# Two-matmul attention scores, recurrence states on 128 rows, a conv norm without its wide reciprocal, and weight low parts made by ScalarE and an accumulating DMA

## The chip, the cores and the metric

The kernel runs on one core of one Trainium2 chip. Its time is the device time of one execution in microseconds (us). Three runs of the kernel before gave 1368.75, 1370.97 and 1372.02 us, a median of 1370.97. The profile shows one further execution, of 1370.76 us, whose span on the engines is 1369.0 us.

## The reference, cut to what matters

Two layers work on a residual stream of 512 tokens by 1024 channels, all in float32. Each layer norms the stream (RMSNorm, modulated by a conditioning vector), projects it to 28 column tiles of 128, runs three token mixers on those tiles, projects the mixers' outputs back, and then runs a gated MLP with a depthwise convolution of width 3.

```python
for l in range(DEPTH):                      # 2 layers
    mod = cond @ w_ada[l] + b_ada[l]        # six shifts, scales and gates
    h = _rmsnorm(x, norm1_w[l]) * (1.0 + sc1) + sh1
    x = x + g1 * _token_mixers(h, ...)      # conv | attention | HGRN2, then w_out
    h = _rmsnorm(x, norm2_w[l]) * (1.0 + sc2) + sh2
    x = x + g2 * _conv_ffn(h, w_up[l], conv_f_w[l], w_down[l])
return _rmsnorm(x, final_norm_w)

# in _token_mixers
a = _depthwise_conv(a_val * sigmoid(a_gate), conv_w, conv_b)      # 256 channels, width 31
a = silu(_layernorm(a, ln_w, ln_b))
att: 6 heads of 64; scores q.k / 8 minus a slope times distance, three dilated windows
rec: 6 heads of 64, both directions; state = decay * state + k^T v, chunk after chunk
return concatenate([a, att, rec]) @ w_out
```

## The kernel before

**Precision.** TensorE's fast type (`float32r`) keeps fewer bits than float32, so every weight and every activation of the large products is split into a high part `hi` (the value rounded to that type) and a low part `lo` (value minus `hi`). A product is then three matmuls, hi·hi, hi·lo and lo·hi, into one PSUM tile (`block`). Weights come from HBM in chunks of 128 rows by up to 1024 columns. `loader` brings them into raw buffers (`wr`, three of them), and `splitter` makes `hi` by a copy on ScalarE or VectorE, whichever the planner thinks sooner done, and `lo` by a subtraction on VectorE. A chunk is split when it lies at most three chunks ahead of the one in use (five for the wide ones).

**Stages.** Each layer has: `first_group`, in which the first column tiles (six) are accumulated at the same time, row block by row block, as the normed activations `h[k]` appear; then one tile after the other (`tile_gemm`, 24 matmuls of 512 columns for 8 row blocks). In the mixers these are the 22 tiles of `REST`, followed by the eight output tiles of `OUT1`, with 12 matmuls each. `last_group` computes the rest of a projection in two halves of 256 tokens, so that the next norm can start on the first half. `first_group` takes the row blocks in halves of 256 tokens too, with a lead of `LAG` = 5 first halves; only in the first layer's mixers is the lead 1. It runs four times in all.

**Mixers.** Beside the tiles run threads: `evac` takes each finished tile out of PSUM; `att` works on a pair of heads with eight `att_tile`s (scores, softmax, transposes); `rec` works on a pair of recurrent heads, with seven levels of small matmuls, then the states and the output; `conv` runs 31 taps on VectorE and then its norm. An `att_tile` takes 64 rows of the pair's `q` and `k`, the rows of its head, and makes the scores with three matmuls (64 rows, 512 columns): hi·hi, hi·lo, lo·hi. `rec` computes each chunk's update `u` for both heads at once as 128 by 128 products, of which it uses the two 64 by 64 diagonal blocks, each on its own 64 rows, in six VectorE instructions for each direction. `conv` spreads the variance over all rows by two products with a constant 128 by 128 matrix, then takes a square root and a reciprocal of 128 by 512 elements.

**Order.** Nothing is scheduled by hand. The Python program is a list of threads with priorities; `run_threads` takes the first one whose needs are met by a clock that adds up estimated costs (`Clock`), and instructions are issued in that order on every engine. The matmuls of the tiles have the lowest priority and fill in. Each engine then runs its own list in order. All loads are issued by SyncE (SP), in one queue, each after the buffer that it overwrites is free; GpSimd (POOL) has almost nothing to do. All of the engines' instructions carry the lines of a few helpers (L181 for VectorE and ScalarE, L274 for matmuls, L280 for transposes, L263 for loads), so the profile is read by tile names: `wh`, `wl` are the parts of a chunk, `hx` the normed activations, `g` and `m` PSUM tiles, `qk` the parts of q and k, `st` the states.

## Time and profile before

| | |
|---|---|
| Median of three runs | 1370.97 us (1368.75 to 1372.02) |
| Profiled execution | 1370.76 us, span 1369.0 us, mean granted TensorE clock 0.991 |
| TensorE matmuls busy | 1344.9 us, 98% of the span |
| VectorE busy | 1070.0 us, 78% |
| ScalarE busy | 609.6 us, 45% |
| GpSimd busy | 2.1 us, 16 instructions |
| DMA | 169.19 MB, 124 GB/s over the span |
| TensorE's waits named in the table of waits | about 17 us in all |

The busy time of an engine is a share of the span, not a proof that it is the bound: matmuls overlap in the array, so a matmul's own duration (about 390 ns for 512 columns) is longer than the distance from one start to the next. In what follows the distance between starts is used as the cost. The span falls into stages: the start up to about 60 us, the first layer's mixers to 317, a half-wise `last_group` and `first_group` around 317 to 373, the MLP to 668, and the same again for the second layer (mixers from 736 to 972, MLP from 1029 to 1324), with the last norm at the end.

### The profile page before, as it was taken

Reading aid. Unit: us, or ns where it says so; the run is one execution under the profiler, and the core shown is the slowest. Engines: PE = TensorE matmul, PEld = TensorE weight load, DVE = VectorE, ACT = ScalarE, POOL = GpSimd, SP = SyncE. Lnnn points to the kernel's source line nnn. Section 1 sums busy time; section 2 is a strip of 40 time slices with the busy share of each in tenths; the row PEclk is TensorE's granted clock in tenths of the full one; section 3 lists DMA queues with packets and bytes.
Section 4 is the critical chain, followed back from the end, with each engine's and each line's share of the span. In section 5 each row is a group of like instructions: output and inputs, shape, how many; then the busy total and the mean of one; then the engine's idle time right before and its main releaser. Section 6 shows DMA issues by size and latency. Waiting matters only on the chain.

```text
span 1369.0 us, 24502 instructions
## 1 busy us (share of the span) xinstructions
PE 1344.9 (98%) x10042; PEld 1112.4 (81%) x10042; DVE 1070.0 (78%) x1841; ACT 609.6 (45%) x1017; POOL 2.1 (0%) x16
## 2 busy tenths in 40 slices
PE   8999999999999999999999999999999999999997
PEld 7977767778988888888899777777898888888887
DVE  6799999898599999766695999888868565556666
ACT  4537556565342433333453473746535232233332
POOL 0000000000000000000000000000000000000000
PEclk8999999999999999999999999999999999999998
DMA  9534443232348788432431312011422323323221
GB/s 353 189 134 142 124 151 94 81 105 89 103 148 293 254 280 290 126 108 70 140 99 63 106 54 99 32 53 54 139 78 57 128 76 95 101 86 122 77 93 63
DMA packets 55264, 169.19 MB, mean 124 GB/s; under 512 B 6256, under 2 KB 8304, under 8 KB 55152
## 3 DMA queue, kind: packets, MB, share of 16 engines
q1 hardware_dynamic: 55152, 167.63, 37.9%
q8 instruction: 79, 1.29, 0.4%
q14 instruction: 33, 0.27, 0.1%
HBM read 165.50 MB, written 2.10 MB: 122 GB/s over the span
## 4 chain that ended last, share of the span: by engine, by line
PE 84%; DVE 12%; ACT 2%; issue 1%; DMA 0%; SPq 0%; DVEq 0%; ACTq 0%
PE m L274 53%; PE g L274 29%; DVE acc L181 2%; PE m L280 2%; DVE KK L181 2%; DVE QQ L181 1%; DVE wl L181 1%; DVE TT L181 1%; DVE wa L181 1%; DVE P L181 1%; DVE hx L181 1%; DVE x L181 1%; DVE st L181 0%; DVE sc L181 0%; DMA x<-xT 0%
## 5 line engine op out<-in xcount | busy, mean ns | idle before, releaser
L274 PE MATMUL g<-hx,wh 128*128 128x512 f32 (+1 forms) x1288 | 402.6, 390 | 0.9 <-DVE qk L181 0.8
L274 PE MATMUL m<-hx,wh 128*128 128x512 f32 (+1 forms) x1136 | 318.0, 364 | 0.0
L181 DVE TENSOR_TENSOR wl<-wr,wh 128x1024 fp32r<-128x1024 f32 (+3 forms) x215 | 220.5, 1027 | 90.4 <-ACT wh L181 79.4
L274 PEld LDWEIGHTS g<-hx,wh 128*128 128x128 f32 x1288 | 237.2, 189 | 53.2 <-issue 7.7
L181 ACT CAST wh<-wr 128x1024 fp32r<-128x1024 f32 (+3 forms) x176 | 157.1, 893 | 250.9 <-PE m L274 155.0
L274 PE MATMUL g<-hx,wl 128*128 128x512 f32 (+1 forms) x648 | 252.7, 390 | 0.0
L274 PEld LDWEIGHTS m<-hx,wh 128*128 128x128 f32 x1136 | 204.3, 189 | 34.2 <-issue 0.6
L274 PE MATMUL m<-hx,wl 128*128 128x512 f32 (+1 forms) x576 | 209.0, 363 | 0.0
L274 PEld LDWEIGHTS g<-hx,wl 128*128 128x128 f32 x648 | 122.5, 189 | 25.4 <-issue 3.8
L274 PEld LDWEIGHTS m<-hx,wl 128*128 128x128 f32 x576 | 108.7, 189 | 16.9
L181 DVE SCALAR_TENSOR_TENSOR x<-m,mod,x 128x256 f32<-128x256 f32 (+1 forms) x112 | 66.2, 592 | 43.1 <-PE m L274 42.1
L181 DVE SCALAR_TENSOR_TENSOR acc<-ap,par,acc 128x512 f32<-128x512 f32 x120 | 89.8, 748 | 2.2
L181 DVE SCALAR_TENSOR_TENSOR tmp<-m,par,tmp 128x511 f32<-128x511 f32 x120 | 89.1, 746 | 1.9
L181 ACT ACTIVATE P<-P,sm 128x512 f32<-128x512 f32 x72 | 51.5, 721 | 42.6 <-DVE sm L181 42.2
L181 ACT ACT_TABLE_LOAD x49 | 62.9, 1283 | 6.0 <-DVE sm L181 4.5
L181 DVE CAST wh<-wr 128x1024 fp32r<-128x1024 f32 (+3 forms) x41 | 24.5, 598 | 52.4 <-PE m L274 37.1
L181 ACT ACTIVATE tmp<-tmp 128x512 f32<-128x512 f32 x44 | 27.8, 632 | 73.1 <-DVE tmp L181 73.0
L181 ACT COPY km<-KK 128x512 f32<-128x512 f32 x30 | 20.5, 683 | 80.2 <-DVE KK L181 58.8
L181 ACT ACTIVATE tmp<-m,par 128x512 f32<-128x512 f32 x60 | 40.7, 686 | 34.5 <-PE m L274 32.8
L181 DVE CUSTOM_DVE_ANT_0 bias<-bias,cb,par 128x1024 f32<-128x1024 f32 x39 | 49.5, 1278 | 2.3 <-DMA bias<-w_ada 2.3
L181 DVE CUSTOM_DVE_ANT_0 wa<-wa,cb,par 128x1024 f32<-128x1024 f32 x39 | 49.9, 1278 | 0.7 <-DMA wa<-w_ada 0.7
L181 ACT ACTIVATE tmp<-x 128x256 f32<-128x256 f32 (+1 forms) x64 | 28.4, 444 | 46.4 <-DVE x L181 42.4
(319 smaller groups left out, 2158.0 us busy)
## 6 DMA issues: line engine op xcount, KB each, us to landing
wr<-w_up SPq DMA_DIRECT2D x76, 512.0 KB, 3.5
wr<-w_in SPq DMA_DIRECT2D x44, 512.0 KB, 3.5
bias<-w_ada SPq DMA_DIRECT2D x39, 512.0 KB, 4.5
wa<-w_ada SPq DMA_DIRECT2D x39, 512.0 KB, 4.0
wr<-w_down SPq DMA_DIRECT2D x32, 320.0 KB, 2.9
wr<-w_down SPq DMA_DIRECT2D x32, 256.0 KB, 2.6
wr<-w_in SPq DMA_DIRECT2D x16, 384.0 KB, 4.4
wr<-w_up SPq DMA_DIRECT2D x16, 384.0 KB, 3.3
```

Of the source, the lines that this page charges most:

```text
L181: r = f(*a, **k)
L274: self.nc.tensor.matmul(out, lhsT=lhsT, rhs=rhs, start=start, stop=stop, **kw)
L280: self.nc.tensor.transpose(out, in_, self.ident)
```

## The change

The diff has six parts. (1) `att_tile`: q is kept per head as a 128-row tile that holds the head's high part on its own 64 rows and its low part on the other 64; k is kept per head with the same 64 rows twice. Two matmuls of 128 rows then give hi·hi + lo·hi and hi·lo + lo·lo. The rows are moved by SBUF-to-SBUF DMAs on the SP queue (`shift`): two of 128 KB for a pair's q, three of 256 KB for its k, of which the third overwrites what the first two read. k takes two `qk` buffers instead of one, and there are three instead of two. (2) `rec`: `u` is computed per head, 64 columns of the array each, so that both heads' blocks lie in the same 64 columns of PSUM; ScalarE copies the first state, two VectorE instructions on 128 rows make the others, and two ScalarE copies put them into the block-diagonal state. The two products for `QQ` become one instruction. (3) `conv`: the variance is reduced to one value per token (16 matmul instructions of one column), the root and reciprocal are taken on those, and a diagonal matrix and two products spread them; the scale and the sigmoid's bias are fused. (4) `splitter`: for the 22 `REST` and 8 `OUT1` chunks of each layer ScalarE writes `lo = -hi`, and a DMA issued by GpSimd adds the raw chunk to it. (5) `first_group` with a lead of 5 takes both halves of blocks 0 to 4, and then blocks 5 to 7 whole, 512 tokens at once. (6) `wr` has five buffers instead of three; the DMA scratch in SBUF is cut to 4096.

```diff
-BUFFERS = dict(wr=(4, 3), wh=(4, 4), wl=(4, 4), hx=(4, 8), qk=(4, 2), ...
+BUFFERS = dict(wr=(4, 5), wh=(4, 4), wl=(4, 4), hx=(4, 8), qk=(4, 3), ...
...
+    def add_dma(self, out, in_):
+        self.nc.gpsimd.dma_start(out=out.bitcast(F32), in_=in_, accum_op=ALU.add)
+        c = self.clk
+        t = max(c.t.get("ADD", 0.0), c.t["PE"], c.written(out) or 0.0) + size(in_) * in_.shape[0] * 4 / 200e3
+        c.t["ADD"] = t
...
+    def shift(self, out, in_):
+        self.nc.sync.dma_start(out=out.bitcast(F32), in_=in_.bitcast(F32))
+        c = self.clk
+        t = max(c.t.get("DMA", 0.0), c.t["PE"], c.written(in_) or 0.0) + size(in_) * in_.shape[0] * 4 / 350e3
+        c.t["DMA"] = t
...
@@ splitter
             lo = self.sb([128, 1024], ["wl"] + more, F32R)[:, :t.shape[1]]
-            self.v.tensor_tensor(out=lo, in0=t, in1=hi.bitcast(F32), op=ALU.subtract)
+            if i in self.by_dma:
+                self.s.activation(lo, hi.bitcast(F32), AF.Copy, scale=-1.0)
+                yield (lo,)
+                self.add_dma(lo, t)
+            else:
+                self.v.tensor_tensor(out=lo, in0=t, in1=hi.bitcast(F32), op=ALU.subtract)
@@ first_group
-        steps = [(k, 0) for k in range(lag)]
-        for k in range(KD):
-            steps += [(k, 1)] + ([(k + lag, 0)] if k + lag < KD else [])
+        if lag > 1:
+            steps = [(k, hf) for hf in range(2) for k in range(lag)] + [(k, None) for k in range(lag, KD)]
+        else:
+            steps = [(k, 0) for k in range(lag)]
+            for k in range(KD):
+                steps += [(k, 1)] + ([(k + lag, 0)] if k + lag < KD else [])
@@ evac, q
+                sc.activation(t, ps.unsqueeze(1).to_broadcast([128, 2, T]), AF.Copy, scale=-0.125)
+                v.scalar_tensor_tensor(lo, ps, -0.125, t[:, 0].bitcast(F32), ALU.mult, ALU.subtract)
+                for hd in range(2):
+                    self.shift(t[own[1 - hd], hd], lo[own[hd]])
@@ evac, k
+                t = [self.sb([128, 2, T], "qk", F32R) for _ in range(2)]
+                self.copy(t[0][:, 0], ps)
+                v.tensor_tensor(out=t[0][:, 1], in0=ps, in1=t[0][:, 0].bitcast(F32), op=ALU.subtract)
+                for hd in range(2):
+                    self.shift(t[1][own[hd]], t[0][own[1]])
+                self.shift(t[0][own[1]], t[0][own[0]])
@@ conv
-        for i in range(2):
-            self.mm(var, self.onesC, sq[i], i == 0, i == 1)
-        self.s.activation(r, var, AF.Sqrt, bias=self.eps)
-        self.v.reciprocal(r, r)
+        self.mean_sq(var, sq, slice(0, T), True, True, self.onesC)
+        d = yield from self.roots(var, slice(0, T))
+        yield from self.spread(r, d)
@@ rec
-                mm(u[:, c], kt[:, c], V[:, c], True, True)
+                for hd in range(2):
+                    r = slice(64 * hd, 64 * hd + 64)
+                    mm(u[r, c, :64], kt[:, c, r], V[:, c, r], True, True, tile_position=(0, 64 * hd))
...
+            self.s.copy(su[:, 0], u[:, seq[0], :64])
+            for i, c in enumerate(seq[1:]):
+                v.scalar_tensor_tensor(su[:, i + 1], su[:, i], TT[:, d, 128 * c:128 * c + 1], u[:, c, :64],
+                                       ALU.mult, ALU.add)
+            for hd in range(2):
+                r = slice(64 * hd, 64 * hd + 64)
+                self.s.copy(st[r, :, r], su[r])
@@ att_tile
-        mm(sp, q[r, 0, s], k[r, 0], True, False)
-        mm(sp, q[r, 0, s], k[r, 1], False, False)
-        mm(sp, q[r, 1, s], k[r, 0], False, True)
+        for i in range(2):
+            mm(sp, q[:, hd, s], k[:, i], i == 0, i == 1)
@@ run
+            by_dma |= set(range(len(ch) - len(REST), len(ch) + KD))
```

More of the change, by code (lines that the diff above doesn't have):

```diff
@@ L69, in span @@
 def span(ap):
[L70 removed]
+    lo = hi = ap.offset % ap.ap[0][0]
     for s, n in ap.ap[1:]:
@@ L271, in dma @@
         c.last[sb.tensor.name] = t + 2.0
+    def add_dma(self, out, in_):
[3 more added lines that the diff above has]
+        c.t["ADD"] = t
+        lo, hi = span(out)
+        l = c.w.setdefault(out.tensor.name, [])
+        l[:] = [e for e in l if not (lo <= e[0] and e[1] <= hi)] + [(lo, hi, t + 3.0, "DMA")]
+        c.last[in_.tensor.name] = c.last[out.tensor.name] = t + 3.0
+    def shift(self, out, in_):
[3 more added lines that the diff above has]
+        c.t["DMA"] = t
+        lo, hi = span(out)
+        c.w.setdefault(out.tensor.name, []).append((lo, hi, t + 2.4, "DMA"))
+        c.last[out.tensor.name] = t + 2.4
     def mm(self, out, lhsT, rhs, start, stop, **kw):
@@ L569, in rstd, with mean_sq @@
         return ps
-    def mean_sq(self, ps, sums, s, first, last):
+    def mean_sq(self, ps, sums, s, first, last, ones=None):
         n = (s.stop - s.start) // 128
@@ L576, in mean_sq @@
                 c = s.start + 128 * i
-                self.mm(ps[:, i:i + 1], t[:, c:c + 128], self.onesD[:, :1], first and i + j == 0,
+                self.mm(ps[:, i:i + 1], t[:, c:c + 128], (self.onesD if ones is None else ones)[:, :1], first and i + j == 0,
                         last and i == n - 1 and j == len(sums) - 1)
@@ L705, in first_group @@
                 yield from self.block(pss[i][:, s], ws[k], i * 128, (h2[:, 0, s], h2[:, 1, s]), k == 0,
-                           k == KD - 1 and hf == 1, start=k == 0 and hf == 0)
-            if hf:
+                           k == KD - 1 and hf != 0, start=k == 0 and hf == 0)
+            if hf != 0:
                 self.give(*ws[k])
@@ L1051, in rec @@
         v.tensor_tensor(out=kd, in0=KK[:, 0], in1=KK[:, 1], op=ALU.add)
-        for d in range(2):
-            v.tensor_tensor(out=QQ[:, d], in0=q, in1=TT[:, 1 - d], op=ALU.mult)
+        v.tensor_tensor(out=QQ, in0=q.unsqueeze(1).to_broadcast([128, 2, T]), in1=TT[:, 1:], op=ALU.mult)
         S = self.sb([128, 2, 4, 128], "S")
@@ L1340, in run @@
         a = self.a
-        ch, wide = [], set()
+        ch, wide, by_dma = [], set(), set()
         for l in range(L):
```

83 lines of the change are left out of this document (41 added, 42 removed).

## The prediction

> **What bounds the kernel now.** The page's busy times come first, then the busy times by stage (columns: start:end, length, then busy time and count of TensorE, weight loads, VectorE, ScalarE, GpSimd, granted clock, DMA share, GB/s): the mixers and the MLP of each layer.
>
> ```profile
> span 1369.0 us, 24502 instructions
> ...
> 60.00:317.00 257.00, 249.48 (x2693) 184.51 (x2691) 230.59 (x441) 150.02 (x267) 0.04 (x1) 0.99 0.38 119
> ...
> 373.00:668.00 295.00, 295.00 (x1309) 244.25 (x1308) 245.39 (x360) 103.50 (x146) 0.00 (x0) 1.00 0.56 186
> ...
> 736.00:972.00 236.00, 234.54 (x2578) 177.58 (x2578) 208.26 (x400) 139.19 (x246) 0.00 (x0) 1.00 0.23 73
> ```
>
> TensorE is without work for 7.5 us of the first mixers, 1.5 of the second and none of the MLP. VectorE is the second engine, at 90% and 88% in the mixers; ScalarE stands at 58% and 59%, GpSimd at nothing. What TensorE waits for is scattered:
>
> ```profile
> PE m L274 <- DVE tmp L181: 3.4, 3, 2.0
> PE g L274 <- DVE TT L181: 3.2, 1, 3.2
> PE m L274 <- DVE sc L181: 2.3, 3, 1.1
> ```
>
> The first two lie in the start and the end, the third in the recurrence. So the time is TensorE's list of matmuls, end to end. A matmul taken from it shortens the kernel by the distance to the next start, and work taken from VectorE gives back at most the 9.0 us of idle TensorE in the mixers. (The granted clock there is 0.99 and 1.00, so there is nothing to win by it.)
>
> **Scores (the large term).** The normal price is the chain's row for a run of tile products; around one score triple the timeline (start, duration) shows another one, and the groups give the number of matmuls:
>
> ```profile
> 538.01 10.88 PE g L274 x48
> ```
> ```profile
> 297.19 0.39 PE L274 MATMUL g<-hx,wl 128*128 128x512 f32 x1
> 297.42 0.40 PE L274 MATMUL g<-hx,wh 128*128 128x512 f32 x1
> 297.75 0.96 PE L274 MATMUL m<-qk,qk 64*128 64x512 f32 x3
> 298.64 0.50 PE L274 MATMUL g<-hx,wh 128*128 128x512 f32 x1
> 298.98 0.55 PE L274 MATMUL m<-vr,S 128*128 128x64 f32 x4
> ```
> ```profile
> L274 PE MATMUL m<-qk,qk 64*128 64x512 f32 x144 | 43.2, 420 | 1.0 <-DVE qk L181 0.3 <-DVE sm L181 0.3 <-ACT tmp L181 0.2
> ```
>
> 48 tile matmuls take 10.88 us: 0.227 each. From 297.42 to 298.98 pass 1.56 us, with two tile matmuls (0.45) and one triple in them: the triple costs 1.10. Its three matmuls as such would be 0.68; the other 0.42 lies at the borders (0.33 before, 0.89 for three, 0.34 after), where the array goes from 128 rows to 64 and back. The 144 matmuls are 48 triples. After the change a tile has two matmuls of 128 rows, in the shape of the tile products, so I give them 0.227 and no border: 0.45. A saving of 0.65, if every triple stood alone, would be 31 us; but in the timeline some triples follow each other or a transpose without a border. A lower estimate without borders inside is the group's own 43.2 us less 96 × 0.227 = 21.8, which is 21.4 us. I take 23.4: the 21.4 and 2 us of the borders that the group's busy time leaves to its neighbours (0.10 before, for some twenty triples). Bounds: one matmul of three goes and the borders stay, 48 × 0.227 = 10.9; every triple alone, 31.
>
> **First groups.** Three of four calls lose their halves for blocks 5 to 7. In the 256-column stretch below 36 matmuls lie between the two starts:
>
> ```profile
> 317.40 0.40 PE L274 MATMUL m<-hx,ap 128*128 128x256 f32 x2
> ...
> 321.71 0.40 PE L274 MATMUL m<-hx,ap 128*128 128x256 f32 x2
> ```
>
> 4.31 / 36 = 0.120, so two halves cost 0.240 against 0.227 whole. Three blocks × 6 tiles × 3 products = 54 pairs for a call: 0.7 us, 2.1 in all. The second half of block 0 is needed after five half blocks, as before; from then on the order asks for one second half every 18 × 0.12 = 2.2 us, where it was one in 4.3. Nothing in the trace waits there (57.00 of 57.00 us busy in the stage from 972 below), so I add nothing; were VectorE late by one second half, 2.2 us a call.
>
> ```profile
> 972.00:1029.00 57.00, 57.00 (x474) 56.90 (x473) 37.42 (x74) 23.82 (x45) 0.00 (x0) 1.00 0.27 82
> ```
>
> **Conv norm.** Removed are two products on constants; added are 16 one-column instructions and two spreading products, priced by the last norm and by a spread of 256 columns:
>
> ```profile
> 249.93 1.98 PE L274 MATMUL m<-tmp,onesC 128*128 128x512 f32 x4
> 251.84 0.66 PE L274 MATMUL m<-wa,cT 128*32 128x128 f32 x16
> ```
> ```profile
> 1359.20 0.61 PE L274 MATMUL m<-onesD,t 128*128 128x1 f32 x4 [0.91 <-DVE t L181]
> 1359.67 0.58 PE L274 MATMUL m<-onesD,tmp 128*128 128x1 f32 x4
> ```
> ```profile
> 341.22 0.61 PE L274 MATMUL m<-t,onesD 128*128 128x256 f32 x2
> 341.48 0.58 PE L274 MATMUL m<-hx,S 128*128 128x256 f32 x2
> 341.90 0.28 PE L274 MATMUL m<-hx,bias 128*128 128x256 f32 x1
> ```
>
> The last fence's third row is read for its start alone. Before: 1.91 us. After: 16 × 0.47 / 4 = 1.88, and two spreads of 0.68 less two halves (0.24), 0.44 each: 2.76. That is 0.85 more a layer, 1.7 in all. TensorE pays so that VectorE is rid of 3.35 us.
>
> **States.** For one direction six instructions become twelve, each with half the array's columns and half the stream. The trace has no such form; its nearest are the products now, and the value products, which work on column halves:
>
> ```profile
> 292.03 0.83 PE L274 MATMUL m<-vr,tmp 128*128 128x128 f32 x6
> 292.61 0.70 PE L274 MATMUL g<-hx,wh 128*128 128x512 f32 x2
> ...
> 158.09 3.65 PE L274 MATMUL m<-PT,va 128*64 128x512 f32 x16
> 161.67 0.53 PE L274 MATMUL m<-qr,km 64*32 64x32 f32 x37
> ```
>
> Now 0.58 us. Sixteen half-array instructions take 3.58, 0.22 each, half of the 0.48 of a full-array one above: the halves run side by side. Twelve thus cost between 0.29 (six pairs, half as long) and 1.16 (one after the other, at the present 0.097). I take 0.66, near the pairs, with a border. × 12 directions: +1.0 us, from −3.5 to +7.
>
> **What VectorE and ScalarE get.** Groups (count | busy, mean ns):
>
> ```profile
> L181 DVE TENSOR_TENSOR wl<-wr,wh 128x1024 fp32r<-128x1024 f32 x123 | 150.2, 1222 | 74.4 <-ACT wh L181 64.6 <-PE m L274 6.0 <-PE m L280 0.3
> L181 DVE TENSOR_TENSOR wl<-wr,wh 128x512 fp32r<-128x512 f32 x48 | 32.9, 686 | 8.9 <-ACT wh L181 8.0
> L181 DVE SCALAR_TENSOR_TENSOR st<-st,TT,m 64x64 f32<-64x64 f32 x48 | 13.4, 280 | 1.6
> L181 DVE COPY st<-m 64x64 f32<-64x64 f32 x24 | 5.3, 219 | 0.5
> L181 DVE RECIPROCAL t<-t 128x512 f32<-128x512 f32 x2 | 6.7, 3348 | 3.2 <-ACT t L181 3.2
> L181 ACT CAST wh<-wr 128x1024 fp32r<-128x1024 f32 x100 | 105.0, 1050 | 146.6 <-PE m L274 96.1 <-PE g L274 36.6 <-DMA wr<-w_up 9.2
> L181 ACT CAST wh<-wr 128x512 fp32r<-128x512 f32 x38 | 23.6, 621 | 42.6 <-PE g L274 21.3 <-PE m L274 21.1
> ```
>
> VectorE loses 22 × 1.22 + 8 × 0.69 = 32.4 us of subtractions a layer, 6 × (2 × 0.22 + 2 × 0.28) = 6 us of states, and 3.35 of reciprocal: 42 of 231 or 208. ScalarE gains 22 × 1.05 + 8 × 0.62 = 28, some 5 for state copies and 3 for the doubled q: 36 on 150 or 139, which makes three quarters of the shorter stage. Neither becomes the bound. This costs TensorE nothing as long as the tile matmuls cover it. I give back nothing of the idle 9.0 us, because the new waits stand against it; −9 is the lower end.
>
> **The new transfers.** Their waits stand in three lists. On ScalarE the negation waits for `hi`, with softmax and the recurrence's copies queued behind it; on GpSimd the adding DMA waits for it, with only other such DMAs behind. On SP the shifts wait for q's or k's low part, and the third k shift for the first two to land; behind it stand loads.
>
> ```profile
> SPq L263 <- DVE wl L181: 829.1, 198, 16.7
> ...
> wr<-w_in SPq DMA_DIRECT2D x44, 512.0 KB, 3.5
> ...
> wr<-w_down SPq DMA_DIRECT2D x32, 256.0 KB, 2.6
> ```
>
> SP mostly waits for free buffers (829 us), and two more are there, so a block of some 5 us in its list is covered by loads made ahead. k is complete two landings (2 × 2.6) after its parts, and V's tile takes 24 × 0.227 = 5.4 us before `att` starts: hidden to within a microsecond. The adding DMA has no row. Its bounds: as a load of its size, 3.5 us, or three times that for its three passes (two reads, one write), 10.5. A chunk is split three chunks ahead, 16 us of TensorE; the chain then is 1.05 + 1.05 + 3.5 to 10.5 = 5.6 to 12.6, hidden either way. I take 5, nearer to the load. For `OUT1` (12 matmuls, 2.7 us a chunk, a lead of 8.2) the chain is 0.6 + 0.6 + 2.6 and up, hidden by less.
>
> By the Trainium skill, "DMA: Bandwidth & Descriptors", section on the anatomy of one DMA, a GpSimd-issued DMA takes about 2.0 us plus its bytes over 436 GB/s; for 512 KB an estimate by that page is 3.2 us, near the load's row, and the sum stays the same.
>
> **Sum**, against the profiled execution's 1370.8 (span 1369.0, 1.8 around it; the median of the runs is 0.2 higher): −23.4 − 2.1 + 1.7 + 1.0 = −22.8, which gives **1348.0 us**.
>
> **Rivals.** *A: the borders stay.* If they belong to the score matmuls and not to the 64 rows, only a matmul of three goes: −10.9 − 2.1 + 2.7, 1360.5. Against it: from one tile, type and PSUM bank to the next the stream keeps its 0.227; only another shape breaks it.
>
> *B: slower; the adding DMAs set the pace.* A layer has 22 of 512 KB and 8 of half that, 26 units, behind each other on one queue. Once a unit takes longer than the mixers' 235 us / 26 = 9.0, TensorE waits for `wl`; the saving is used up at 9.5 (2 × 26 × 0.5 = 26 us). At 10.5, three passes one after the other, each layer's mixers take 273 us, that is 28 and 49 more than 245 and 224: 1425. For it: nothing in the trace shows GpSimd issuing into a busy kernel. Against it: the same bytes as a load land in 3.5, and the DMA share in the mixers is 0.38 and 0.23.
> The same list can be late another way: VectorE may shut GpSimd out while it works. VectorE is busy 230.6 of 257 us; with 42 given back and 12 taken from the stage it leaves 56 us a layer for writing the descriptors of 30 transfers, 1.9 each. From 2.25 each on the saving is used up (30 × 0.38 = 11.4 a layer); at 2.8 a layer is 28 us longer, 1404. GpSimd has 0.04 and 0.00 us in the mixers' rows above, so no row speaks to it, and it stays within B's chance.
> [...]
>
> *C: the waits eat a third.* The first mixers' idle 7.5 us lie mainly in the recurrence and after its last tile, where no filler is left; what the eight scores of the last pair save there (8 × 0.49 = 3.9 a layer) is then waiting, and one landing of 2.6 in excess for some of the six pairs makes up to 15.6. 1348 + 7.8 + up to 7.8: 1356 to 1364. For it: the planner's clock lets the third shift land too early. Against it: VectorE's 42 us free the same chains.
>
> **Chances.** Forecast 0.65, A 0.11, C 0.14, B 0.10. The low end is the forecast with all 9.0 us of idle time gone and the states at −3.5 in place of +1.0: 1334.5, rounded to 1335; the high end is C's, 1364, and A lies inside. B is left out, with the forecast's and C's own tails. Runs of this kernel tell about 0.2% (2.7 us) from nothing: below 1368.2 lie the forecast, A and most of C, 0.87; B at units just over 9 us and C's end give 0.05 for no change; the rest of B is 0.08.
>
> **What would show it.** Score matmuls of 128 rows, 96 of them, at 0.227 from start to start without borders (A: 0.33 and more); TensorE still over 97% busy in the mixers, in 245 and 224 us; VectorE there near 190 us, ScalarE near 185. B would show TensorE waiting for a DMA into `wl`; C, waits on `qk` after a DMA or on `hx` before the last group. The MLP stages should stay at 295 us. A time above 1368 would refute the reading that TensorE's list is the time.

## The result, and the profile after

The changed kernel takes 1380.68 us (median of six, 1374.85 to 1381.69) against 1371.49 us (1368.75 to 1372.29) of the kernel before: a ratio of 1.0062, 95% interval 1.0043 to 1.0080. It is 0.6% slower, where 1348.0 was forecast. Its profiled execution took 1380.60 us, span 1378.8.

First the busy times by stage, in the columns of the prediction's first fence, over the same stretches of time.

```profile
60.00:317.00 257.00, 233.45 (x2671) 179.10 (x2670) 197.35 (x399) 163.01 (x288) 23.40 (x29) 0.95 0.68 173
373.00:668.00 295.00, 294.88 (x1301) 243.87 (x1300) 240.40 (x352) 102.67 (x144) 0.00 (x0) 1.00 0.56 185
736.00:972.00 236.00, 226.09 (x2586) 176.35 (x2585) 176.09 (x361) 151.95 (x260) 23.18 (x29) 0.99 0.55 133
```

The MLP is as full as before. In these stretches of the mixers VectorE fell from 230.6 to 197.4 us and from 208.3 to 176.1 (over the whole execution from 1070.0 to 1010.6), but TensorE is now without work for 23.6 and 9.9 us where it was 7.5 and 1.5, the granted clock of the first stretch fell from 0.99 to 0.95, and the DMA share rose from 0.38 and 0.23 to 0.68 and 0.55. The table of TensorE's waits (total us, times, longest) names two that did not exist:

```profile
PE m L295 <- DMA qk<-qk: 13.3, 3, 7.7
PE m L295 <- DMA wa<-w_sh: 8.5, 3, 3.9
PE g L295 <- DVE TT L181: 3.3, 1, 3.3
...
PE g L295 <- issue: 2.5, 1, 2.5
```

The first is the scores waiting for copies of rows, the second a product waiting for a piece of the modulation's weights; the third, in the start, is as before; the last, in the second layer's mixers, stands before a product with `wl`, and the trace names nothing that ended it. The timeline of SP and of TensorE around the longest of them (start, duration):

```profile
182.31 7.85 SPq L286 DMA_DIRECT2D qk<-qk  x3
190.22 2.22 SPq L263 DMA_DIRECT2D bias<-bias  x2
192.53 1.17 SPq L263 DMA_DIRECT2D wa<-w_sh  x1
```
```profile
195.25 1.22 PE L295 MATMUL m<-qk,qk 128*128 128x512 f32 x2 [7.67 <-DMA qk<-qk]
196.27 1.05 PE L301 MATMUL m<-ident,tmp 128*128 128x128 f32 x4
196.97 2.05 PE L295 MATMUL m<-qk,qk 128*128 128x512 f32 x4
```

SP issues the first two copies of k at 182.3 and then stands, until 190.2, at the third, which overwrites what those two read. Everything behind it in SP's list (the bias, the weights, raw chunks) is as late. TensorE stands 7.7 us, and the first two scores that follow take 1.22 us, where two take 0.62 in the fence further down: the array runs at half clock. SP's own waits and the landings (KB each, median us to landing):

```profile
SPq L263 <- DVE wl L181: 505.0, 140, 18.6
SPq L263 <- DMA wl<-wr: 293.7, 47, 18.2
...
SPq L286 <- DMA qk<-qk: 31.5, 8, 5.9
```
```profile
wr<-w_in SPq DMA_DIRECT2D x44, 512.0 KB, 4.4
wl<-wr POOLq DMA_DIRECT2D x44, 512.0 KB, 5.4
...
qk<-qk SPq DMA_DIRECT2D x18, 256.0 KB, 4.7
```

A raw buffer is free only when the adding DMA that reads it has landed, so loads wait 293.7 us in SP's list for those DMAs. With the 505.0 us for VectorE's subtractions that makes 799, where SP waited 829 us for the subtractions before: SP does not wait longer for buffers than it did, but it now has the copies in the same list. A copy of 256 KB lands in 4.7 us (median of 18), and the 512 KB weights that took 3.5 us take 4.4. For a pair of heads, the time from the issue of k's first copy to the landing of its third is 10.3 us on average over the six pairs in this trace (9.0 to 12.9).

What was paid for did arrive. The scores in the timeline and as a group:

```profile
285.46 0.40 PE L295 MATMUL g<-hx,wh 128*128 128x512 f32 x1
285.69 0.62 PE L295 MATMUL m<-qk,qk 128*128 128x512 f32 x2
286.15 0.40 PE L295 MATMUL g<-hx,wh 128*128 128x512 f32 x1
```
```profile
L295 PE MATMUL m<-qk,qk 128*128 128x512 f32 x96 | 32.4, 440 | 15.0 <-DMA qk<-qk 13.3 <-DVE sm L181 0.8 <-DVE va L181 0.5
```

A tile's score costs 0.46 us from start to start, with no border before or behind it. To separate the list from the waits, I gave every matmul of each trace the usual distance to the next one (the median over all traces here, by the two shapes) and summed; "beyond" is what the real distances, from the first matmul to the last, have on top. The split depends on how the matmuls are grouped: by shape alone it is 1282.5 and 76.0 us before and 1258.6 and 109.3 after, by shape and tile names 1298.8 and 59.7, and 1273.4 and 94.4. The differences hold within 2 us.

| kernel | list, us | beyond, us |
|---|---|---|
| before | 1296.6 | 62.0 |
| after | 1271.4 | 96.4 |

The list became 25.2 us shorter (the sum had 22.8) and the time beyond it grew by 34.4. The question is where the 34.4 come from.

### The profile page after: what moved, and what is told of

Read it like the earlier page. It is cut to its first block, busy times and chain, and to the rows that moved or that the text cites. A ratio compares the mean times of both kernels' runs of the same rounds, so it can differ in the third digit from the quotient of the medians.

```text
span 1378.8 us, 24562 instructions
## 1 busy us (share of the span) xinstructions
PE 1329.9 (96%) x9936; PEld 1103.4 (80%) x9936; DVE 1010.6 (73%) x1767; ACT 652.8 (47%) x1074; POOL 54.2 (4%) x76
## 4 chain that ended last, share of the span: by engine, by line
PE 83%; DVE 8%; DMA 5%; ACT 1%; issue 1%; SPq 0%; DVEq 0%; ACTq 0%
PE m L295 52%; PE g L295 29%; DVE acc L181 3%; PE m L301 2%; DMA qk<-qk 2%; DMA wa<-w_sh 1%; DVE wa L181 1%; DVE KK L181 1%; DVE QQ L181 1%; DMA wa<-w_ada 1%; DVE tmp L181 1%; DVE TT L181 1%; DVE P L181 0%; DVE x L181 0%; DMA x<-xT 0%
## 5 line engine op out<-in xcount | busy, mean ns | idle before, releaser
L295 PE MATMUL m<-hx,wh 128*128 128x512 f32 (+1 forms) x1152 | 327.0, 368 | 0.0
L181 ACT CAST wh<-wr 128x1024 fp32r<-128x1024 f32 (+3 forms) x177 | 155.8, 881 | 260.3 <-PE m L295 165.6
L295 PEld LDWEIGHTS g<-hx,wh 128*128 128x128 f32 x1264 | 233.3, 190 | 51.5 <-issue 5.2
L295 PE MATMUL g<-hx,wl 128*128 128x512 f32 (+1 forms) x628 | 246.1, 392 | 2.5 <-issue 2.5
L295 PEld LDWEIGHTS m<-hx,wh 128*128 128x128 f32 x1152 | 208.8, 189 | 35.8 <-issue 0.4
L181 DVE TENSOR_TENSOR wl<-wr,wh 128x1024 fp32r<-128x1024 f32 (+3 forms) x151 | 151.8, 1007 | 77.0 <-ACT wh L181 72.2
L181 DVE SCALAR_TENSOR_TENSOR x<-m,mod,x 128x256 f32<-128x256 f32 (+1 forms) x108 | 63.4, 587 | 45.2 <-PE m L295 44.1
L181 DVE SCALAR_TENSOR_TENSOR tmp<-m,par,tmp 128x511 f32<-128x511 f32 x124 | 92.4, 747 | 2.0
L275 POOL DMA_DIRECT2D wl<-wr x60 | 52.1, 868 | 913.5 <-ACT wl L181 805.6
L181 ACT ACTIVATE P<-P,sm 128x512 f32<-128x512 f32 x70 | 50.2, 721 | 40.9 <-DVE sm L181 40.4
L181 ACT ACTIVATE wl<-wh 128x1024 fp32r<-128x1024 f32 (+1 forms) x60 | 56.5, 941 | 4.4 <-DVE wh L181 3.3
```

Source lines behind the costliest of these rows:

```text
L181: r = f(*a, **k)
L275: self.nc.gpsimd.dma_start(out=out.bitcast(F32), in_=in_, accum_op=ALU.add)
L295: self.nc.tensor.matmul(out, lhsT=lhsT, rhs=rhs, start=start, stop=stop, **kw)
```

## The experiments

Times are medians against the kernel before on the same chip (1370.4 to 1371.2 us). "Mixers" is, from the trace, the time from the last 256-column matmul of the first group to the first of `last_group` in layer 0, and from the MLP's `last_group` to the mixers' own in layer 1: 250.2 and 292.2 us before, 261.7 and 293.9 after. Each edit changes what the planner sees, and so the order of the whole list; differences of a few us between two variants are not given to an edit unless a row names the cause. Executions of one variant lie up to 10 us apart (three matmuls again: 1365.99 to 1376.08 in twelve), those of the kernel before up to 4 us in 23, and a trace shows one execution.

### Copies of rows and adding DMAs, each undone

**No adding DMA** (VectorE subtracts again):
```diff
-        self.queue_chunks(ch, wide, by_dma)
+        self.queue_chunks(ch, wide, set())
```

> The changed kernel with the low parts of all chunks made by VectorE again (no ScalarE negation, no adding DMA); everything else as changed. Theory A (the adding DMA is the cause: it keeps the raw buffers longer, so SP stands at the next weight load with the moves and loads behind it, and it crowds the DMA engines): TensorE's waits on DMA (22 us in the changed kernel) nearly vanish and with them the half clock, 1347 to 1353 us. Theory S (the cause is k's chain of moves, the third waiting on SP for the landing of the first two): the landings of the moves fall from 4.7 us towards 2.6, but there are still two in a row, so about half of the 13.3 us on qk and of the half clock stays: 1358 to 1366 us. Theory P (the planner's order happens to be worse): waits of another kind, 1365 or more.

1365.2 us, ratio 0.9959 (0.9947 to 0.9971). Mixers 244.0 and 292.4. The copies land sooner (8.1 us on average from a pair's first issue to its third landing, instead of 10.3), and the waits for copies shrink:

```profile
qk<-qk SPq DMA_DIRECT2D x18, 256.0 KB, 3.5
```
```profile
PE m L295 <- DMA qk<-qk: 5.8, 5, 2.0
```

**Three matmuls again, adding DMAs kept:**
```diff
-        for i in range(2):
-            mm(sp, q[:, hd, s], k[:, i], i == 0, i == 1)
+        mm(sp, q[r, 0, s], k[r, 0], True, False)
+        mm(sp, q[r, 0, s], k[r, 1], False, False)
+        mm(sp, q[r, 1, s], k[r, 0], False, True)
```

> The changed kernel with the attention scores of before (three matmuls on 64 rows, no moves of q and k); the adding DMA and everything else as changed. The scores' 23 us of TensorE come back. Theory S: without moves the SP queue is as before and the adding DMA is hidden, so the time is that of before, 1368 to 1373 us. Theory A: the late loads (8.5 us on wa) and their half clock stay without the saving, 1380 to 1390 us.

1369.03 us, ratio 0.9993 (0.9978 to 1.0009), mixers 246.3 and 296.0. Beside the old scores the adding DMAs cost nothing against the kernel before, though the modulation's weights still come late in the table of waits:

```profile
PE m L295 <- DMA wa<-w_sh: 3.9, 3, 3.1
```

**Two independent copies for k:** the evacuation writes each head's half straight into its own buffer, so that no copy waits for another.
```diff
-                self.copy(t[0][:, 0], ps)
+                for hd in range(2):
+                    self.copy(t[hd][own[hd], 0], ps[own[hd]])
...
-                for hd in range(2):
-                    self.shift(t[1][own[hd]], t[0][own[1]])
-                self.shift(t[0][own[1]], t[0][own[0]])
+                for hd in range(2):
+                    self.shift(t[hd][own[1 - hd]], t[hd][own[hd]])
```

> The changed kernel, with k's parts written straight to the two places where they stay (rows 0-63 into the first head's tile, rows 64-127 into the second's, two instructions of 64 partitions each for hi and lo), and two moves of 256 KB that don't depend on each other in place of three of which the last waits. The adding DMA stays. Theory S: the waits on qk (13.3 us) and their half clock go, 1358 to 1363 us. Theory A: SP is late all the same, 1372 to 1381 us.

1364.33 us, ratio 0.9949 (0.9937 to 0.9961). The wait for copies is gone from TensorE's table:

```profile
PE m L295 <- DVE sc L181: 4.7, 7, 1.5
PE m L295 <- DMA wa<-w_sh: 4.6, 2, 3.5
PE m L295 <- DVE tmp L181: 3.9, 4, 2.0
PE m L301 <- DVE P L181: 3.8, 2, 2.0
```

Beside the adding DMAs the chained third copy cost 16.4 us. The copies themselves land no sooner (256 KB in 5.1 us), but the second of the two lands 6.4 us on average after the first is issued, instead of 10.3 for three. So it is the chain and the blocked list, not the single transfer.

**Both** (independent copies, no adding DMA):

> Both of the former: no adding DMA, and two independent moves for k. Theories A and S alike: neither suspected wait is left, and the saving of TensorE's list shows, 1346 to 1350 us. Theory P: 1360 or more, with waits that have nothing to do with DMA.

1367.95 us, ratio 0.9984 (0.9975 to 0.9993): some 18 us more than expected. No wait of TensorE for a DMA is left above 0.5 us, and its waits for VectorE (P 3.9, sc 2.8) stay. Without adding DMAs, undoing the chain gained nothing (1365.2 with it). So the transfers were one cause of two.

### What is left, in four directions

**The small parts alone** (states, conv norm, first groups, buffers; three matmuls and VectorE's subtraction as before, both edits above together):

> The changed kernel with the scores as before (three matmuls of 64 rows, no copies of rows) and with VectorE's subtraction for every weight: what is left of the change is the recurrence states on 128 rows, the norm of the convolution, the first groups and the larger buffers. Theory S (the small parts cost and give what the prediction's sum has for them, -2.1 +1.7 +1.0): 1370 to 1373 us, no difference from the kernel before. Rival (the states' new chain of ScalarE, VectorE and ScalarE holds the recurrence up, and the chain holds TensorE): 1375 to 1381, with the recurrence of pair 0 ending later than in the kernel before (its last products start at 125.4 there).

1376.49 us, ratio 1.0045 (1.0029 to 1.0060): the rival's time. Parts that the sum had at +0.6 cost 5.7. Its sign did not come: in the profiled execution (1372.72 us) pair 0's first output product starts at 125.6 us, where it was 125.4. The distance from the last score product to that product is longer, though, 22.8 us on average over six pairs instead of 13.0.

The six kernels with all the small parts side by side (us):

| scores | VectorE subtracts | adding DMAs |
|---|---|---|
| three matmuls, no copies | 1376.49 | 1369.03 |
| two matmuls, chained copies | 1365.20 | 1380.68 |
| two matmuls, independent copies | 1367.95 | 1364.33 |

The adding DMAs gain 7.5 and 3.6 us, except beside the chained copies, where they cost 15.5. The new scores gain 8.5 to 11.3 us without adding DMAs, and 4.7 with them when the copies are independent; 23.4 was taken. So the loss of some 16 us needs the chain and the adding DMAs together, and the rest of what is missing does not lie in the transfers.

**Adding DMAs only in layer 1:**
```diff
-            by_dma |= set(range(len(ch) - len(REST), len(ch) + KD))
+            by_dma |= set(range(len(ch) - len(REST), len(ch) + KD)) if l else set()
```

> Scores with two independent copies of rows, and the adding DMAs only in layer 1; layer 0 subtracts on VectorE. Theory W (in layer 0 the SP queue, held by loads into raw buffers that wait for an adding DMA, brings the modulation's weights late, and TensorE then stands and runs at half clock): layer 0's mixers 244 to 249 us as in the two runs without adding DMAs (244.0 and 248.6), layer 1's mixers 285 to 287 as in the run with both (285.4): 1358 to 1363 us. Rival (VectorE's work is what counts, and in layer 0 it comes back): 1364 to 1368.

1366.81 us, ratio 0.9971 (0.9960 to 0.9983). Mixers 247.6 and 287.2, as that theory has it for each stage, but the MLP after the first mixers is 369.0 instead of 363.5, and the total goes to the rival.

**Order of tiles:**
```diff
-        Z_F + 1, Z_B + 1, Q_REC + 1, I_REC + 1, G_REC + 1, Q_ATT + 1, ...
+        Q_REC + 1, I_REC + 1, G_REC + 1, Z_F + 1, Z_B + 1, Q_ATT + 1, ...
```

> Scores with two independent copies and adding DMAs in both layers; the order of the projection tiles changed: the three tiles of pair 1 that need no buffer of the recurrence (its query, input and gate) stand ahead of the two forget tiles, which wait until the recurrence of pair 0 frees its buffers. Theory F (TensorE runs out of tiles there, since two forget tiles hold both accumulators, and the products behind a softmax have nothing before them): the waits of 2.2 and 1.9 us at 131 and 134 and the half clock behind them go, layer 0's mixers 242 to 246 us instead of 250.6, layer 1's 283 to 286: 1354 to 1359 us. Rival (the recurrence of one pair after the other is the longest chain, and tiles moved ahead of it only run out later): 1363 to 1368.

1364.97 us, ratio 0.9960 (0.9948 to 0.9972). The waits at 131 and 134 went, layer 0 took 245.4, and layer 1 gave it back with 292.0.

**The planner told landings near the measured ones:**
```diff
-(lo, hi, t + (4.5 if eng is self.nc.gpsimd else 2.4), "DMA")
+(lo, hi, t + (4.5 if eng is self.nc.gpsimd else 4.4), "DMA")
...
-(lo, hi, t + 3.0, "DMA")
+(lo, hi, t + 5.0, "DMA")
...
-(lo, hi, t + 2.4, "DMA")
+(lo, hi, t + 5.0, "DMA")
```

> Scores with two independent copies and adding DMAs in both layers; the planner that writes TensorE's list is told landings near the measured ones (loads 4.4 us after their transfer's end instead of 2.4, copies of rows and adding DMAs 5.0 instead of 2.4 and 3.0). Theory P (the waits come from a list that puts work where its data hasn't landed): the waits for the modulation's weights (4.6 us in the run with the old figures) and the half clock behind them go, 1355 to 1360 us. Rival (SP is blocked for longer than any fixed figure, and no list puts that right): the wait for those weights stays at 3 us or more, 1363 to 1367.

1367.27 us, ratio 0.9968 (0.9956 to 0.9981). The wait for the modulation's weights did go from the table, and layer 0 took 242.6, the least so far; layer 1 took 295.9. Both theories of one late load fail in the sum: what one stage gains, the other loses. Only the planner's figures differ here from the kernel with independent copies, so its order alone moves the time by some 3 us (2.9).

### The recurrence's states

In the timeline, what lies between the updates of the states and the first output product of pair 0, before (first fence) and in the kernel before with the new states alone (second):

```profile
117.16 0.83 PE L274 MATMUL m<-vr,tmp 128*128 128x128 f32 x6
118.52 0.83 PE L274 MATMUL m<-vr,tmp 128*128 128x128 f32 x6
119.07 0.47 DVE L181 COPY st<-m 64x64 f32<-64x64 f32 x2
119.57 1.21 DVE L181 SCALAR_TENSOR_TENSOR st<-st,TT,m 64x64 f32<-64x64 f32 x4
122.69 0.47 DVE L181 COPY st<-m 64x64 f32<-64x64 f32 x2
123.19 1.22 DVE L181 SCALAR_TENSOR_TENSOR st<-st,TT,m 64x64 f32<-64x64 f32 x4
125.41 0.66 PE L274 MATMUL m<-vr,S 128*128 128x64 f32 x4
```
```profile
117.50 0.57 PE L274 MATMUL m<-vr,tmp 128*64 128x64 f32 x12
118.87 0.20 ACT L181 COPY tmp<-m 128x64 f32<-128x64 f32 x1
121.75 0.59 DVE L181 SCALAR_TENSOR_TENSOR tmp<-tmp,TT,m 128x64 f32<-128x64 f32 x2
123.37 0.72 ACT L181 COPY st<-tmp 64x192 f32<-64x192 f32 x2
124.31 0.57 PE L274 MATMUL m<-vr,tmp 128*64 128x64 f32 x12
126.65 0.19 ACT L181 COPY tmp<-m 128x64 f32<-128x64 f32 x1
129.50 0.59 DVE L181 SCALAR_TENSOR_TENSOR tmp<-tmp,TT,m 128x64 f32<-128x64 f32 x2
133.99 0.69 ACT L181 COPY st<-tmp 64x192 f32<-64x192 f32 x2
134.86 0.95 PE L274 MATMUL m<-vr,S 128*128 128x64 f32 x4
```

8.3 us became 17.4. The work is less (for one direction 0.59 us of VectorE where it was 0.47 + 1.21), but it is handed over twice between ScalarE and VectorE, at each hand-over behind other work in the receiving list, and the second direction's products (124.31) are planned only when the first direction's states are ready. From the last score product to the first output product, 13.0 us on average over the six pairs became 24.4.

**The changed kernel with the states as before:**
```diff
-                    mm(u[r, c, :64], kt[:, c, r], V[:, c, r], True, True, tile_position=(0, 64 * hd))
+                mm(u[:, c], kt[:, c], V[:, c], True, True)
...
-            self.s.copy(su[:, 0], u[:, seq[0], :64])
+                        v.tensor_copy(st[r, i, r], u[r, c, r])
```

> The changed kernel with the states of the recurrence computed as before (128 by 128 products, six VectorE instructions for each direction without a hand-over). In every run with the new states about 20 us lie between the last score product of a recurrence and its first output product (19.6 for pair 0 of the changed kernel), against 13.0 in the kernel before. Theory R (the three recurrences follow each other through their single buffers, and the new states, with ScalarE, VectorE, ScalarE in turn and the second direction behind the first, lengthen each by some 8 us; tiles run out before the last one ends): the distance returns to 12 to 14 us and the time falls to 1368 to 1374. Rival D (the dependent copies of rows and the late weights set the changed kernel's time, and the recurrence has room): 1378 to 1382 us, whatever the distance.

1384.3 us (four executions, 1377.95 to 1387.41), ratio 1.0109 (1.0094 to 1.0124). The distance fell to 13.6 us on average over six pairs, and the time did not: theory R falls for the changed kernel. Waits for copies are still 15.3 us there.

**The same with independent copies:**

> Scores with two independent copies of rows, adding DMAs in both layers, and the states as before. Theory R: both losses are gone, distance 12 to 14 us, 1346 to 1357 us. Rival D (nothing but the copies counted, and they are mended already): 1362 to 1366 us as without this edit.

1362.09 us, ratio 0.9942 (0.9929 to 0.9955), where the new states had 1364.33 and 0.9949 (0.9937 to 0.9961): the intervals overlap, and the 2.2 us are not clear of noise. Distance 12.9 on average. The profiled execution took 1366.70 us, more than that median.

**The kernel before with the new states and nothing else** (the second fence above):

> The kernel before with the new states and nothing else of the change. Theory R: the distance in the recurrence rises from 13 to about 20 us and more, and the time to 1376 to 1382 us. Rival (in the kernel before there are tiles enough to cover a longer recurrence): 1369 to 1373 us.

1375.47 us, ratio 1.0035 (1.0023 to 1.0047): the states alone cost 4.8 us there, most of what the small parts cost together.

**New products, but all on VectorE without a hand-over:**
```diff
-            self.s.copy(su[:, 0], u[:, seq[0], :64])
-            yield (su[:, 0],)
+            v.tensor_copy(su[:, 0], u[:, seq[0], :64])
...
-            yield (su[:, 1:],)
-                self.s.copy(st[r, :, r], su[r])
+                v.tensor_copy(st[r, :, r], su[r])
```

> Scores with two independent copies, adding DMAs in both layers; the states from the new products of half the columns, but all on VectorE without a hand-over: a copy, two multiply-adds, two copies for each direction, issued one behind the other, so that the second direction's products need not wait for the first direction's states. Theory H (the hand-overs between ScalarE and VectorE lengthen the recurrence, not the products): distance 13 to 15 us, 1348 to 1358. Rival (the products on half the array, or the detour through a buffer of 128 rows, are what is slow): distance 18 us or more, 1362 to 1366 us.

1365.06 us, ratio 0.9958 (0.9946 to 0.9971). The distance is 13.2 us on average: the hand-overs make it long, with the second direction's products waiting behind them, and not the products (theory H). But the time is that of the kernel with independent copies alone. The longer recurrence cost 4.8 us where VectorE also has the subtractions; with the adding DMAs undoing it gave nothing clear of noise in either form, and a loss of 3.6 in the changed kernel itself.

### What holds the mixers

All of these are made on the kernel with independent copies and the states as before, 1362.1 us. Its trace is of the execution of 1366.70 us, so that differences from this trace come out larger than those of the medians.

**40 us fewer in TensorE's list:**
```diff
-        self.mm(ps, wh[:, s], al, False, False)
+        if not (getattr(self, "thin", False) and c0 // 128 % 2):
+            self.mm(ps, wh[:, s], al, False, False)
```

> On the kernel with independent copies, adding DMAs and the old states (1362.1 us): the projection tiles of the mixers leave out the product of the weights' high part and the activations' low part for every second row block, so that this part of the computation is missing. That takes 22 tiles x 4 matmuls x 0.227 = 20.0 us a layer from TensorE's list, 40 in all, and leaves every other chain as it is. Theory L (the list sets the time, and the waits are single delays that don't depend on it): 1320 to 1327 us. Theory C (the chains of softmax and recurrence set the mixers' end, and tiles only fill): less than half of it comes, 1345 to 1360, and TensorE's waits for VectorE and ScalarE grow to 40 us and more.

1352.74 us, ratio 0.9869 (0.9855 to 0.9883): theory C, though the named waits for VectorE and ScalarE stayed well below the 40 us expected with it. Of 40 us in the list, 9.4 arrived. In the traces the mixers became 5.8 and 10.0 us shorter (241.1 and 281.1), and the stage from the first layer's `last_group` to the MLP's became 5.1 us longer (369.0 instead of 363.9). (`thin` is set while the tiles of `REST` run.) The two mixers' stages of the kernel that it is made from, and of this one:

```profile
64.00:312.00 248.00, 236.27 (x2652) 181.48 (x2651) 207.14 (x427) 165.32 (x282) 22.82 (x28) 0.97 0.69 181
675.00:967.00 292.00, 285.23 (x2986) 231.03 (x2985) 227.21 (x468) 181.64 (x301) 26.30 (x32) 0.99 0.52 131
```
```profile
62.00:304.00 242.00, 219.90 (x2561) 166.58 (x2559) 206.45 (x426) 163.35 (x276) 22.72 (x28) 0.96 0.70 186
672.00:954.00 282.00, 268.25 (x2897) 216.07 (x2896) 226.07 (x467) 182.48 (x303) 26.46 (x32) 0.99 0.56 137
```

TensorE's idle time went from 18.5 to 35.9 us. VectorE is busy for 85% and 80% of the two. By the sum over lists, the list is 1236.0 us instead of 1275.2, and 104.9 instead of 78.8 us lie beyond it.

**Fifteen of 31 convolution taps fewer for VectorE:**
```diff
-        for i in range(1, CW):
+        for i in range(1, 16):
```

> On the same kernel: 16 of the convolution's 31 taps, 15 left out for both tiles, so that this part of the computation is missing. VectorE loses 2 x 15 x 0.76 = 22.8 us a layer; TensorE's list is the same. Theory V (VectorE's load lengthens the chains that TensorE waits for): its waits for VectorE in the mixers fall from 12.7 to 6 or less, 1348 to 1355 us. Rival (the chains are long by their hand-overs, or the waits are not what costs): 1359 to 1363 us.

1362.52 us, ratio 0.9941 (0.9929 to 0.9952): nothing came. The taps' 45 us left VectorE's list, but its busy time fell only from 1024.4 to 993.1 us, because the planner gave it more of the copies. These 31 us of VectorE's load do not set the time.

**A second buffer for keys and decays:**
```diff
-BUFFERS = dict(wr=(4, 5), ... KK=(4, 1), ... TT=(6, 1), ... t2=(2, 2))
+BUFFERS = dict(wr=(4, 3), ... KK=(4, 2), ... TT=(6, 2), ... t2=(2, 1))
```

> On the same kernel: two buffers instead of one for the recurrence's keys and decays (paid for by two raw buffers and one of the small ones), so that the forget tiles of the next pair are taken out of PSUM while the recurrence of this pair still runs. Theory B (the single buffers put one recurrence behind the other and leave both accumulators held): pair 1's first scores start 10 us or more before the 95 us after pair 0's that the kernel has now, and the time is 1348 to 1355 us. Rival (that order is not what costs): 1359 to 1365 us.

1373.4 us, ratio 1.0025 (1.0014 to 1.0036), mixers 245.4 and 295.2. Pair 1 starts 89 us after pair 0 instead of 95, not 85. With three raw buffers the MLP behind the first mixers takes 369.0 us and waits for a weight's low part (4.7 us), so the two raw buffers given up are in the result too; the buffers of the recurrence did not pay for them.

**The modulation's loads on GpSimd's queue:**
```diff
-                w.append(self.ada_load(l, order[i + len(w)], tags))
+                w.append(self.ada_load(l, order[i + len(w)], tags, None if l else self.nc.gpsimd))
```

> On the same kernel: in layer 0 the loads of the modulation's weights are issued by GpSimd instead of SP, away from the loads that wait for raw buffers. Theory W (SP, blocked by loads that wait for an adding DMA, makes these weights late): the waits for them (4.4 us, 3.7 at most) and the half clock behind them go, 1352 to 1358 us. Rival (they are late in any queue, or other waits take their place): 1360 to 1365 us.

1374.13 us, ratio 1.0025 (1.0014 to 1.0036). The wait for these weights fell from 4.4 to 1.0 us; in its place, from the tables of TensorE's and GpSimd's waits:

```profile
PE m L295 <- DVE wl L181: 5.1, 1, 5.1
PE m L295 <- ACT S L181: 4.3, 2, 3.6
```
```profile
POOL wa L263 <- DVE mod L181: 48.7, 10, 12.0
POOL wa L263 <- PE m L295: 47.6, 3, 42.5
```

The loads now block GpSimd's list for 48.7 and 47.6 us, with adding DMAs behind them. The waiting moved from one list to the other.

**Five levels of seven in the recurrence:**
```diff
         for lev in range(7):
+            if lev in (1, 2):
+                h *= 2
+                continue
```

> On the kernel with independent copies, adding DMAs and the old states (1362.1 us): the recurrence leaves out two of its seven levels, so that this part of the computation is missing. A level takes about 4.3 us from scores to scores (five levels from 76.7 to 98.4 in the first pair), so each recurrence is some 8.7 us shorter, 26 a layer; from TensorE's list go 64 matmuls of 11 ns a level, 8.4 us in all. Theory K (the three recurrences, one after the other, set the mixers' end): 1330 to 1345 us. Theory L (what counts is the list): 1352 to 1355. Rival (the recurrence has room): 1357 to 1363 us.

1354.47 us, ratio 0.9879 (0.9863 to 0.9895). 7.6 us came, close to what leaves TensorE's list (8.4 expected, 8.0 by the sum over lists), where a chain of recurrences would have given 17 and more. The edit shortens the list and the recurrence at once (pair 0 takes 40.4 us from its first scores to its first output product instead of 52.2), so the time alone does not tell which of them gave it.

**A third buffer for the softmax:**
```diff
-BUFFERS = dict(... P=(2, 2), ... t2=(2, 2))
+BUFFERS = dict(... P=(2, 3), ... t2=(2, 1))
```

> On the same kernel: three instead of two buffers for the softmax (paid for by one of two small buffers that the norms use). Theory A (the attention's chain from scores to transposes, two tiles at a time, holds TensorE where tiles have run out): the waits of TensorE's transposes for the softmax go, pair 0's attention ends earlier than at 165.6 us, 1352 to 1358 us. Rival (other chains take their place): 1360 to 1364 us.

1357.71 us, ratio 0.9907 (0.9892 to 0.9922): 4.4 us better, and the fastest here but for two of the kernels that leave work out. Pair 0's attention ends at 159.6 us instead of 165.6. TensorE's table no longer has a wait of the transposes for the softmax (1.0 us in the profile of the kernel that it is made from), so the removed waits are too small to be the gain as such, and 5.0 us of waits for copies stand there instead of 0.4. The profiled execution took 1354.89 us, less than the median, and half clock is nearly absent in it:

```profile
60.00:317.00 257.00, 244.53 (x2763) 193.27 (x2762) 216.81 (x443) 167.37 (x291) 24.22 (x29) 0.99 0.69 183
736.00:972.00 236.00, 231.07 (x2577) 182.07 (x2577) 191.12 (x390) 155.49 (x267) 22.68 (x26) 1.00 0.57 139
```

The granted clock is 0.99 and 1.00 where it was 0.97 and 0.99, and 66.1 us lie beyond the list of 1276.3. But the clock is not the gain: over the whole span its mean is 0.986 to 0.996 in the five executions and 0.991 to 0.997 in the six of the kernel that this one is made from. What gave the 4.4 us is not shown.

## Why the prediction was wrong

**TensorE's list is the time (failed).** This is the step that decided. The prediction named 1368 us as what would refute it, and 1380.7 does. Shortening the list by 25.2 us gave 7 with independent copies, shortening it by 40 more gave 9.4. The reading that fits both is that the tiles in the list had covered the chains of softmax and recurrence beside them, and no longer do; that is argued, and no run isolates it. In "What VectorE and ScalarE get", "I give back nothing of the idle 9.0 us" was the term: the time beyond the list rose from 62.0 to 78.4 us even with independent copies, and to 96.4 in the changed kernel. Two levels of the recurrence gave 7.6 us, near the 8.0 that they occupy in the list, but they shorten the chain too. Which of the chains holds which part stays open: neither VectorE's load (0 us for 31) nor the length of the recurrence (nothing clear of noise for 8 us a pair, with adding DMAs) does by itself.

**The new transfers (failed).** "Hidden to within a microsecond" had two landings of 2.6, so 5.2 us; measured are 10.3 on average from first issue to last landing, and 8.1 without the adding DMAs. "A block of some 5 us in its list is covered by loads made ahead" was 7.85 us at its longest, and TensorE waited 13.3 us for copies. Beside the adding DMAs the chained copy cost 16.4 us, without them nothing. Rival C had the mechanism ("the planner's clock lets the third shift land too early") and not the size: it allowed 7.8 us.

**The half clock (missing).** "There is nothing to win by it" held, but there was something to lose. The clock records of the profiled executions show half speed for 3.4 us of the mixers before and for 30.7 us after (17.1 with independent copies). The scores behind the 7.7 us wait, above, are among them. An estimate from these records: the 27.3 us more at half speed put off at most 13.7 us of the list. It is not the whole loss: the changed kernel's execution with the highest mean clock, 0.993, still took 1374.85 us, where the profiled one of the kernel before took 1370.76 at 0.991. By the Trainium skill, "TensorE: Matmul & The Clock Gate", Part 1 on the HAM clock gate, an idle window of some 3.4 us puts the array at half clock. The changed kernel's trace agrees in kind, its four long records being 6.8, 10.2, 6.8 and 6.8 us and each beginning within a wait of TensorE of 3.1 to 7.7 us; its two waits of 2.5 us are followed by none. The other traces do not bear out a length at which it starts: half clock begins within waits of 1.9 us (the kernel before with the new states) and 1.8 us (independent copies), in the kernel before with no wait over 0.2 us in the six us ahead of it, and a wait of 3.1 us (three matmuls again) is followed by none. So a wait can be paid for a second time, but how long it must be is not shown.

**States (TensorE's price wrong in sign, the chain left out).** The twelve products take less than the 0.58 us of before, 0.50 from start to start in the timeline; 0.66 was taken.

```profile
296.88 0.57 PE L295 MATMUL m<-vr,tmp 128*64 128x64 f32 x12
297.38 0.73 PE L295 MATMUL g<-hx,wh 128*128 128x512 f32 x2
```

What they cost is in the hand-overs: 8.3 us became 17.4 between products and output, which no term had, and it cost 4.8 us in the kernel before.

**Right.** The scores: 96 matmuls, no border, and a list shorter by 25.2 us with all parts (22.8 in the sum). That the two agree is in part luck: between kernels that differ in the scores alone (old scores against chained copies, with and without adding DMAs) the list is 18 to 20 us shorter, where 23.4 was taken, and the other 4 to 6 lie in the small parts, where the sum had +0.6. The Trainium skill, "TensorEngine Tiling (Array Packing)", Key Properties, has TensorE drained when the tiling mode changes; that agrees with the 0.33 and 0.34 us at the borders of a 64-row triple before and with their absence now. The adding DMA: 5.4 us, where 5 was taken (the estimate of 3.2 beside it was too low), and without harm by itself (1369.03). The MLP: 294.9 us of 295, and from its `last_group` start to the next 362.4 us instead of 363.2 in layer 1, where 0.7 was the first group's term. The conv norm was not measured by itself. Rival A is refuted by the 0.46, rival B by the absence of any named wait for `wl` in the mixers; the one of 2.5 us before a product with `wl` has no cause in the trace. GpSimd issues an adding DMA in 0.87 us, mean of 60, most of them in stretches where VectorE is busy for 77% and 75%:

```profile
L275 POOL DMA_DIRECT2D wl<-wr x60 | 52.1, 868 | 913.5 <-ACT wl L181 805.6 <-DMA wr<-w_in 19.4 <-ACT PT L181 18.8
```

The rule of the Trainium skill, "SBUF — State Buffer", section on who interferes with whom, that VectorE's copies, casts and `tensor_scalar` can shut GpSimd out of descriptor writing, does not show as a cost here: the 1.9 us that a transfer could take are not reached.

**VectorE and ScalarE (both put too far).** VectorE's busy time fell by 59 us, where two layers of 42 were given, and ScalarE's rose by 43 (609.6 to 652.8), where two of 36 were. The subtractions (69 us less) and the reciprocal went as counted. Part of the difference is that the planner gave copies and casts to VectorE that ScalarE had made (10 us more of them there, although the states' 5 us are gone). Over the first mixers themselves, from 63 to 325 us, VectorE is busy for 202 us and ScalarE for 164, where 190 and 185 were given.

## What to carry to other kernels

An engine that is 98% busy because filler covers the waits of other chains is not simply the bound: take a known amount from its list in a throwaway kernel and see how much arrives, before a change is priced by that list. Price a new step by its hand-overs, each behind whatever stands in the receiving engine's list, and not by its busy time alone. In a queue that issues in order, a transfer that waits for another transfer makes everything behind it late, so prefer independent copies to chained ones. Here the chain cost 16.4 us beside the adding DMAs and nothing without them: test two new transfers together as well as one by one.

## What the runs showed of the hardware

Landings depend on what runs beside them: a 256 KB copy within SBUF took 3.5 us (chained) and 4.6 (in pairs) without adding DMAs and 4.7 (chained) and 5.0 to 6.1 (in pairs) with them, a 512 KB load of the mixers' weights 3.5 us before, 4.0 and 4.1 with the copies alone and 4.4 and 4.6 with the adding DMAs too (medians). An adding DMA within SBUF took 5.4 us for 512 KB and 4.3 for 256 KB in the changed kernel. Moving a load to another engine's list freed the one list and blocked the other, and cost 12.0 us. In the changed kernel every wait of TensorE of 3.1 us and more came with half clock for 6.8 to 10.2 us, in which two score matmuls took 1.22 us instead of 0.62; in other traces here shorter waits did so too, and one of 3.1 us did not. A triple of 64-row matmuls among 128-row ones cost 0.33 and 0.34 us from start to start at its borders instead of 0.23; two of 128 rows had no border.
